# Transposes by age, five and six early blocks, and down's rows and residual tiles between units

## The chip, the core and the metric

The kernel runs on one core of a Trainium2 chip. The metric is the device time of one execution in microseconds (us). Before the change it is 2997.43 us, the median of three runs (2996.47 to 3000.92).

## What is computed

A diffusion trunk of two layers over 1024 latent tokens and, in the first layer only, 256 context tokens, model width 1024. Cut to what matters here:

```python
for l in range(2):
    p, qn, kn, vn, qg, kg, vg = project(x * (1 + s1) + sh1, w_in[l])
    mix = concat([pool(p), neighbourhood_attention(...), blocked_gqa(...)]) @ w_out[l]
    x = layer_norm(alpha * x + g1 * mix, ln1_g[l], ln1_b[l])
    ffn = conv_ffn(x * (1 + s2) + sh2, w_up[l], conv_w[l], conv_b[l], w_down[l])
    x = layer_norm(alpha * x + g2 * ffn, ln2_g[l], ln2_b[l])
    # layer 0: the same for the context stream xc

def conv_ffn(h, w_up, conv_w, conv_b, w_down):
    acc = conv3(h @ w_up) + conv_b          # along the tokens
    a, g = split(acc, 2)                    # 2816 columns each
    return (a * silu(g)) @ w_down
```

## The kernel before

All products are fp32 by three passes: each operand is split into a high and a low part (a cast on ScalarE, ACT, line L176 or L170, and a subtraction on VectorE, DVE, L177 or L172), and TensorE (PE) multiplies high by high, high by low and low by high. So each weight tile passes DMA, ACT and DVE before PE can use it. SyncE (SP) issues nearly all transfers in order; a transfer that waits for a tile holds those behind it. GpSimd (POOL) does some elementwise work.

A layer runs as: adaLN and in-projection, the three head groups, the out-projection with the first layer norm (class `OutProj`), `up` of the feed-forward part, `down` with the second layer norm. Layer 0 then runs the context stream's feed-forward part (`ffn`).

**Out-projection.** `OutProj.run` multiplies token tiles of 128 rows, 48 matmuls of 128x512 for each, into the PSUM tile `oacc` (L1072). PSUM holds four tiles of that size. The first tiles run k-major. `norm` of a tile multiplies by the gate into `s` (L1082, `SBUFS` buffers), sums with DVE (`ln_add`, L231), takes the variance on ACT and the power on POOL, applies it on ACT (L246), multiplies by the gain on POOL (L262), adds the offset on DVE (L263) to give `xm`, and stores `s` to DRAM (`XS`). Then PE transposes `xm` in eight matmuls of 128x128 into `tps` (L252), which takes one of the same four PSUM tiles. `follow` decides when the transposes stand in PE's order, and starts norms while fewer than `NXM` are not yet transposed.

**Early blocks.** `up` is a seven-product (Strassen-like) scheme, class `UpLat`. It needs sums of the transposed tiles named T1, T2 and T4, made from latent tiles 4 to 7 in `OutProj.sums`; they go to DRAM (`TX2`, `TX14`) and are loaded again in `enter`. Two of the products (24 of a block's 84 matmuls) need only the first four tiles. For `AHEAD` blocks they run ahead, as `early` (tile `oe`), while the last tiles are normed and transposed. `end` writes the order out by hand: "T" is a transpose, "E" an early block. Results of early blocks 2 and up go to DRAM (`UE`) and return before their block. The first product that needs a sum is `o<-T2`, which starts `up` proper.

**Down.** `DownLat.run` does seven products of 11 units; a unit loads a half tile of the hidden state (L1586) and one of the weights (L1592), splits both, and runs 12 matmuls. Between units it pops work from `self.later`. The residual tile is loaded (`s<-XS`, L1645 for tiles 0 to 3, L1655 for 4 to 7), multiplied by a row and added to another on DVE (`residual`, L1735, whose operations the trace gives to the helper's line L1329). The rows (`ln_g`, `ln_b`, `g`; in layer 1 also `l2g` and `l2b`) are loaded ahead of `run` (L224). A scheduler places instructions; what is not pinned may go earlier.

**Context feed-forward part.** `ffn` ends with `ln_add` and `modulate_T` for two tiles, then `tps`, then layer 1's projection.

Of the kernel before, what the change touches and what calls it, by code (L numbers as in the profile page):

```python
# [19 lines left out]
DEPTH = 2  # L20
# [13 lines left out]
NXM = (2, 3)  # L34
# [11 lines left out]
AHEAD = (4, 4)  # L46
# [30 lines left out]
YQ = 1  # L77
# [20 lines left out]
def trunk_kernel(ctx, tc, a, out):  # L98
# [51 lines left out]
    UE = {(l, f): dram.tile([P, 1024], F32, name=f"UE{l}{f}") for l in range(DEPTH) for f in range(2 * NP)}  # L150
    TX2 = dram.tile([4, P, 512], F32, name="TX2")
    TX14 = dram.tile([4, P, 1024], F32, name="TX14")
# [75 lines left out]
    def ln_add(s, o, pool, junk, apply=True):  # L228
# [6 lines left out]
        nc.vector.tensor_scalar(out=nm, in0=sm, scalar1=-1.0 / D, scalar2=None, op0=ALU.mult)  # L235
        sq = pool.tile([P, 1], F32, tag="lsq", name="lsq", bufs=LNB)
# [85 lines left out]
    def project_begin(l, wx1, ps, z, xt):  # L322
# [8 lines left out]
        for k in range(8):  # L331
            for i in range(len(accs)):
                accum_mm(xt, i, uA, 512, accs[i], k)
# [713 lines left out]
    class OutProj:  # L1047


        def __init__(self, l, units, op, ps):  # L1050
            self.l, self.units, self.op, self.ps = l, units, op, ps
            self.xs, self.stored, self.side = None, [], None
            self.rows = {}
            self.silu = False
            self.norms, self.late = [], []
# [21 lines left out]
        def norm(self, z, mx, t, acc, xin, x1_dst):  # L1077
# [6 lines left out]
            ln_add(s, xt, op, xt)  # L1084
            if SILU and not self.silu:
# [3 lines left out]
            sink = (lambda pt: self.sums(mx, t - 4, pt)) if z.lat and t >= 4 else None  # L1089
            self.late.append(  # L1090
                modulate_T(
                    s, G, B, op, "xm", NXM[self.l], self.ps, mx[0][:, t], mx[1][:, t], ident, False, mul=nc.gpsimd,
                    sink=sink,
                )
            )
            (nc.scalar if XQ else nc.sync).dma_start(out=x1_dst[t * P:(t + 1) * P, :], in_=s)

        def sums(self, mx, t, pt):
# [16 lines left out]
            else:  # L1115
                self.stored.append(t)
                nc.sync.dma_start(out=TX2[t], in_=r[:, hi])
                nc.sync.dma_start(out=TX14[t][:, lo], in_=q[:, lo])
            tt(nc.gpsimd, q[:, hi], q[:, hi], r[:, hi], ALU.subtract)
            nc.sync.dma_start(out=TX14[t][:, hi], in_=q[:, hi])  # L1120
# [8 lines left out]
        def run(self, z, tiles, mx, xin, x1_dst, kmajor=False, hold=False):  # L1129
# [5 lines left out]
            if kmajor:  # L1135
                for t in tiles:
                    acc(t)
                for k in range(7):
                    for t in tiles:
                        self.product(mx, accs[t], t, k)  # L1140
                    if self.side:
                        self.side()
            for t in tiles:
                if kmajor:
                    self.product(mx, accs[t], t, 7)
                else:
                    acc(t)
                    for k in range(8):
                        self.product(mx, accs[t], t, k)
                self.norms.append((z, mx, t, accs[t], xin, x1_dst))  # L1150
                if not kmajor and not (hold and t == tiles[-1]):
                    self.follow()
            if kmajor:
                while self.norms and len(self.late) < NXM[self.l]:
                    self.norm(*self.norms.pop(0))

        def end(self, cover, steps):

            while self.norms:
                self.norm(*self.norms.pop(0))  # L1160
            for x in steps:
                (self.late if x == "T" else cover).pop(0)()
# [43 lines left out]
    def ffn(l, z, mx, fp, ffp, ps, cols, g2, background, x1, lnrows, tail, ready, end=None, firstp=None):  # L1206
# [50 lines left out]
        def down(g, fs, F, last):  # L1257
            units = [wunit(a["wdown"][l, f], scale=g2) for f in fs[:3]]
            units += [wunit(a["wdown"][l, f], pool=fp, scale=g2, tags=("tmp", "tmp"), bufs=nb) for f in fs[3:]]
            for t in range(nt):  # L1260
# [24 lines left out]
                else:  # L1285
                    direct = end and t >= DIRECT
                    r = ln_add(s, o, fp, fp.tile([P, D], BF16, tag="junk", name="junk"), not direct)
                    tail(t, s, *(r or ()))
# [42 lines left out]
    class UpLat:  # L1331
# [36 lines left out]
        def enter(self, fu, xs, stored, background, t4=lambda fu: quarters(fu, ("T4",))[0]):  # L1368

            self.fu, self.xs, self.background = fu, xs, background  # L1370
            v = lambda x: x.rearrange("p (k j) -> p k j", k=4)

            def x(src):
                t = fu.tile([P, 1024], F32, tag="cv", name="xt", bufs=CVB)
                nc.sync.dma_start(out=t[:, :src.shape[1]], in_=src)
                return t
            xs.append(t4(fu))
            for t in stored:
                y = x(TX2[t])
                split(xs[1][0][:, t], xs[1][1][:, t], v(y[:, 0:512]))  # L1380
                y = x(TX14[t])
                split(xs[0][0][:, t], xs[0][1][:, t], v(y[:, 0:512]))
                split(xs[2][0][:, t], xs[2][1][:, t], v(y[:, 512:1024]))
            for t in range(4):
                if t not in stored:
                    y = x(TX14[t][:, 512:1024])
                    split(xs[2][0][:, t], xs[2][1][:, t], v(y[:, 0:512]))
# [6 lines left out]
        def weights(self, f, first=False):  # L1394
# [5 lines left out]
            elif b["early"] is None:  # L1400
                b["early"] = self.uf.tile([P, 1024], F32, tag="ue", name="ue", bufs=2)
                nc.sync.dma_start(out=b["early"], in_=UE[self.l, f])
                b["u1"] = b["early"][:, lo]
# [10 lines left out]
        def early(self, i):  # L1414
# [6 lines left out]
            u = self.uf.tile([P, 1024], F32, tag="ue", name="ue", bufs=2)  # L1421
            nc.scalar.copy(u[:, 0:512], o[:, 0:512])
            self.mm(o[:, 512:1024], a_, 512, "B21", True)
            tt(nc.vector, u[:, 512:1024], o[:, 512:1024], u[:, 0:512], ALU.add)
            self.blocks[f] = {"early": u, "u1": u[:, 0:512]}
# [758 lines left out]
```

## Time and profile before

| what | value |
|---|---|
| median of three runs | 2997.43 us |
| profiled execution, its own time | 2999.13 us |
| its span | 2997.4 us |
| mean granted clock of PE | 0.971 |
| PE, DVE, ACT, POOL busy | 93%, 76%, 50%, 33% |
| out-projection to `up`, layer 0 | 610 to 801 us |
| `down`, layer 0, start | about 1251 us |
| out-projection to `up`, layer 1 | 2188 to 2328 us |
| `down`, layer 1, start | about 2777 us |

The profile gives for each stretch the busy time of each engine, PE's granted clock (1.00 is 2.4 GHz, 0.50 would be 1.2 GHz all the time) and the DMA share. "Waits" lists for whom an engine was idle. A timeline row gives start, length, engine, line, operation and, in brackets, the idle time ahead and what ended it.

### The profile page before, as it was taken

To read this page: it belongs to the slowest core of one execution; us is meant where nothing else is said; L and a number is where in the kernel's file an instruction comes from. 1 tells how busy PE (TensorE), PEld (TensorE's weight loads), DVE (VectorE), ACT (ScalarE), POOL (GpSimd) and SP (SyncE) were. 2 spreads that over 40 slices of the span, in tenths; PEclk is the share of its full clock that TensorE was granted. 3 is DMA by queue.
4 is the path that set the end of the run, shared out by engine and by line. 5 is a ranking of instruction groups with operands and counts; after the bars stand their busy time and mean duration, and the time that the engine had idled before them with its cause. 6 is when DMAs were issued, how large, how long until landed. Compare 5 with 4: busy or idle time off the path is not lost.

```text
span 2997.4 us, 41914 instructions
## 1 busy us (share of the span) xinstructions
PE 2784.9 (93%) x14715; PEld 2359.7 (79%) x14715; DVE 2285.8 (76%) x3651; ACT 1492.3 (50%) x2328; POOL 991.3 (33%) x773
## 2 busy tenths in 40 slices
PE   8998889988799999899799799999998899999898
PEld 6798778977578887788788679888987688887676
DVE  4985789956688888756887765699957788887667
ACT  4222888824344444434655422598854444444343
POOL 0304354114345554200253440353133444553001
PEclk9999999998899999999899999999999999999999
DMA  7786662164554444865555588452134444445773
GB/s 275 249 269 192 184 169 85 43 219 154 190 168 155 154 152 158 292 211 185 181 177 183 186 269 289 142 171 83 58 121 137 161 158 158 157 159 179 264 222 129
DMA packets 271686, 531.08 MB, mean 177 GB/s; under 512 B 26778, under 2 KB 110834, under 8 KB 270708
## 3 DMA queue, kind: packets, MB, share of 16 engines
q1 hardware_dynamic: 270180, 524.11, 53.9%
q10 hardware_dynamic: 1296, 4.29, 0.4%
q8 instruction: 117, 1.92, 0.3%
q14 instruction: 93, 0.76, 0.1%
HBM read 394.16 MB, written 134.14 MB: 176 GB/s over the span
## 4 chain that ended last, share of the span: by engine, by line
PE 25%; DVE 15%; DMA 10%; issue 4%; ACT 4%; POOL 2%; SPq 1%; POOLq 0%; DVEq 0%; ACTq 0%
PE o L1363 7%; PE dy L1605 4%; PE dx L1605 3%; DVE wl L177 2%; PE pvs L848 2%; PE oacc L1072 2%; PE s L786 2%; DVE wl L172 2%; PE pt L803 1%; DVE s L1329 1%; DMA raw<-in_wup_dram 1%; DMA wm<-in_wmT_dram 1%; DMA VD<-stB 1%; DMA raw<-in_wdown_dram 1%; DVE w L1329 1%
## 5 line engine op out<-in xcount | busy, mean ns | idle before, releaser
L1329 POOL TENSOR_TENSOR cv<-cv 128x512 f32<-128x512 f32 (+1 forms) x110 | 251.5, 2286 | 262.5 <-DVE cv L1499 126.5
L1363 PE MATMUL o<-mxh,wh 128*128 128x512 f32 x640 | 253.5, 397 | 19.3 <-DVE cv L1499 12.7
L177 DVE TENSOR_TENSOR PT<-pt,PT 128x512 fp32r<-128x512 f32 (+2 forms) x396 | 247.8, 644 | 18.4 <-ACT PT L176 16.2
L1363 PE MATMUL o<-mxl,wh 128*128 128x512 f32 x640 | 252.6, 395 | 0.0
L1363 PE MATMUL o<-mxh,wl 128*128 128x512 f32 x640 | 251.6, 394 | 0.0
L786 PE MATMUL s<-K,q 128*128 128x256 f32 (+2 forms) x960 | 236.8, 359 | 14.6 <-DVE m L753 12.8
L176 ACT CAST wh<-raw 128x512 fp32r<-128x512 f32 (+1 forms) x132 | 119.0, 906 | 216.7 <-PE o L1363 141.1
L794 ACT ACTIVATE P<-P,m 128x1280 f32<-128x1280 f32 (+3 forms) x216 | 221.9, 1028 | 9.5 <-DVE m L753 8.0
L177 DVE TENSOR_TENSOR wl<-raw,wh 128x512 fp32r<-128x512 f32 (+1 forms) x132 | 162.8, 1239 | 75.7 <-ACT wh L176 75.1
L176 ACT CAST PT<-pt 128x512 fp32r<-128x512 f32 (+2 forms) x396 | 205.4, 558 | 26.0 <-PE pt L834 10.4
L848 PE MATMUL pvs<-PT,V 128*128 128x256 f32 (+1 forms) x1488 | 209.9, 289 | 5.0 <-DVE PT L177 2.0
L318 PE MATMUL pacc<-wh,mxh 128*128 128x512 f32 (+1 forms) x512 | 191.8, 375 | 15.5 <-DVE rt L284 7.2
L753 DVE CUSTOM_DVE_ANT_0 P<-s,zero,m 128x512 f32<-128x512 f32 (+1 forms) x288 | 189.0, 656 | 20.7 <-PE s L786 1.1
L172 DVE TENSOR_TENSOR wl<-raw,wh 128x1024 fp32r<-128x1024 f32 (+1 forms) x112 | 151.9, 1367 | 62.4 <-ACT wh L170 61.9
L848 PEld LDWEIGHTS pvs<-PT,V 128*128 128x128 f32 x1488 | 186.2, 191 | 12.2 <-ACT mixr L859 4.6
L320 PE MATMUL pacc<-wh,mxl 128*128 128x512 f32 (+1 forms) x512 | 187.5, 367 | 2.2 <-DVE mxl L177 2.2
L319 PE MATMUL pacc<-wl,mxh 128*128 128x512 f32 (+1 forms) x512 | 187.6, 366 | 0.0
L176 ACT CAST wh<-hw 128x1024 fp32r<-128x1024 f32 x98 | 102.7, 1053 | 160.8 <-PE dx L1605 37.5
L177 DVE TENSOR_TENSOR wl<-hw,wh 128x1024 fp32r<-128x1024 f32 x98 | 125.1, 1286 | 75.2 <-ACT wh L176 74.7
L170 ACT CAST wh<-raw 128x1024 fp32r<-128x1024 f32 (+1 forms) x118 | 119.1, 1018 | 93.4 <-POOL raw L168 23.6
L786 PEld LDWEIGHTS s<-K,q 128*128 128x128 f32 x960 | 140.8, 190 | 29.4 <-DVE m L753 23.1
L803 PE MATMUL pt<-ident,P 128*128 128x128 f32 x1032 | 160.1, 273 | 3.5 <-DVE PT L177 2.5
(355 smaller groups left out, 7849.1 us busy)
## 6 DMA issues: line engine op xcount, KB each, us to landing
raw<-in_wup_dram SPq DMA_DIRECT2D x140, 512.0 KB, 4.7
wm<-in_wmT_dram SPq DMA_DIRECT2D x96, 512.0 KB, 4.9
w<-in_wdown_dram SPq DMA_DIRECT2D x44, 512.0 KB, 3.7
hw<-in_wdown_dram SPq DMA_DIRECT2D x66, 256.0 KB, 3.7
q<-QN SPq DMA_DIRECT2D x96, 128.0 KB, 3.1
q<-QG SPq DMA_DIRECT2D x96, 128.0 KB, 2.7
TD0T<-w SPq DMA_DIRECT2D x44, 256.0 KB, 2.2
hw<-HD0S SPq DMA_DIRECT2D x44, 256.0 KB, 3.2
```

The lines of the kernel that those rows point to most:

```text
L172: (sub or nc.vector).tensor_tensor(out=lo[:, :n], in0=raw[:, :n], in1=h[:, :n], op=ALU.subtract)
L176: nc.scalar.copy(h, src)
L177: nc.vector.tensor_tensor(out=lo, in0=src, in1=h, op=ALU.subtract)
L318: nc.tensor.matmul(acc[:, :n], lhsT=xh[:, i, k, :], rhs=wh[:, o:o + n], start=(k == 0), stop=False)
L753: nc.vector.tensor_tensor_reduce(out=dst, in0=src, in1=bias, scale=-1.0, scalar=init, op0=ALU.add, op1=ALU.min, accum_out=m)
L786: nc.tensor.matmul(s[:, :n], lhsT=q[:, part, c0:c0 + P], rhs=K[:, k0:k0 + n], start=(part == 0), stop=(part == 1))
L794: nc.scalar.activation(out=self.P, in_=self.P, func=AF.Exp, bias=self.m, scale=-1.0, accum_out=self.rsum())
L803: nc.tensor.transpose(pt[:, b, :], self.P[:, p0 + b * P:p0 + (b + 1) * P], ident)
L848: nc.tensor.matmul(self.pv[:, c0:c0 + n], lhsT=V[:, vb, :], rhs=x[:, sl, c0:c0 + n], start=(self.c == 0), stop=(self.c == self.tot - 1),)
L1329: eng.tensor_tensor(out=out, in0=a_, in1=b_, op=op)
L1363: nc.tensor.matmul(o, lhsT=lhsT, rhs=rhs, start=fresh and k == 0 and i == 0, stop=k == 3 and i == 2, skip_group_check=not fresh,)
L1605: nc.tensor.matmul(o, lhsT=x[:, tc_], rhs=w[:, r], start=fresh and j == 0 and i == 0, stop=j == NP - 1 and i == 2, skip_group_check=not fresh,
```

## The change

- `OutProj`: `NXM` becomes 3 in both layers. `follow` is called in the middle and at the end of a tile and releases a transpose that is three steps old (`AGE`). The last latent tile and the context tiles take another route through the norm: the gain on DVE as soon as the mean is known, then one offset on DVE, instead of ACT, POOL and DVE in turn.
- `AHEAD` is (5, 6); all but one early block go through DRAM in halves of 512 columns, with `UEB` (3, 4) half buffers. The first half is stored from ACT's queue. "X" in `end` is `take`, which loads T1 and T2 while the early blocks run; `enter` loads T4 alone.
- `DownLat.run`: rows, then residual tiles 0 to 3, are loaded between units of product 1; tiles 4 to 7 in product 3; the residual operations run between units of products 2 and 4. Loads and operations are pinned in program order. Layer 1's `l2g` and `l2b` are asked for in the last norms, and the scheduler puts them into product 1.
- The context part's tail takes the gain and offset route. The stores of `YN` go from ACT's queue to SP's.
- The matmuls are the same in number.

```diff
-NXM = (2, 3)
+NXM = (3, 3)
-AHEAD = (4, 4)
+AHEAD = (5, 6)
+AGE = 3
+UEB = (3, 4)
-YQ = 1
+YQ = 0
...
+            if z.lat and t < 7:
+                ln_add(s, xt, op, xt)
+                f = modulate_T(s, G, B, op, "xm", NXM[self.l], self.ps, *dst, ident, False, mul=nc.gpsimd, sink=sink)
+            else:
+                xm = op.tile([P, D], F32, tag="xm", name="xm", bufs=NXM[self.l])
+                nm, rs = ln_add(s, xt, op, xt, False, lambda nm: gain(xm, s, nm, G))
+                offset(xm, xm, rs, B)
...
+                f = lambda: transpose_T(xm, self.ps, *dst, ident, False, sink)
+            self.late.append((self.step, f))
...
-        def follow(self, keep=1):
-            while len(self.late) > (keep if len(self.norms) < 2 else 0):
-                self.late.pop(0)()
+        def follow(self):
+
+            self.step += 1
+            if self.late and self.step - self.late[0][0] >= AGE:
+                self.late.pop(0)[1]()
             while self.norms and len(self.late) < NXM[self.l]:
                 self.norm(*self.norms.pop(0))
...
+        def take(self, proj, xs):
+
+            self.xs = proj.xs = xs
+            for t in proj.stored:
+                y = rawp.tile([P, 1024], F32, tag="raw", name="xt")
+                nc.sync.dma_start(out=y, in_=TX12[t])
+                for i in range(2):
+                    split(xs[i][0][:, t], xs[i][1][:, t], y[:, 512 * i:512 * i + 512].rearrange("p (k j) -> p k j", k=4))
...
-            return [lambda i=i: self.early(i) for i in [*range(2, n), 0, 1]]
+            return [lambda i=i: self.early(i) for i in [*range(1, n), 0]]
...
-                proj.end(up.cover(), "TETEETE")
+                proj.end(up.cover(), "ETEXTEEE")
...
-                proj.end(up.cover(), "ETEETE")
+                proj.end(up.cover(), "EXTEETEEE")
...
-                if j % 2 and self.later:
+                if (j % 2 or j and p in (1, 3)) and self.later:
                     self.later.pop(0)()
...
+            pin = tc.keep_in_program_order
+
+            def fetch(t):
+                return lambda: pin(nc.sync.dma_start(out=s[t], in_=x1[t * P:(t + 1) * P, :]))
             self.product(0, X, True, after=lambda t: nc.scalar.copy(u[t], X[t]))
-            self.later = [lambda t=t: residual(s[t]) for t in range(4)]
+            rows = {}
+            self.later = [
+                lambda: rows.update(ln=self.rows()), lambda: rows.update(g2=self.g2())
+            ] + [fetch(t) for t in range(4)]
...
+            self.later += [lambda t=t: residual(rows["ln"], s[t]) for t in range(4)]
             self.product(2, X, False, after=c11)
-            self.later = [lambda t=t: residual(s[t]) for t in range(4, 8)]
+            self.later += [fetch(t) for t in range(4, 8)]
...
+            self.later += [lambda t=t: residual(rows["ln"], s[t]) for t in range(4, 8)]
             self.product(4, X, True, after=c22)
```

PE's order where layer 0's out-projection transposes its first tiles. Before, the two transposes come after five tiles of `oacc`:

```order
2560 L1072 MATMUL oacc<-wh,mxh 128x512 x2
2561 L1072 MATMUL oacc<-wl,mxh 128x512 x2
2562 L1072 MATMUL oacc<-wh,mxl 128x512 x2
2563 L252 MATMUL tps<-ident,xm 128x128 x16
2564 L1072 MATMUL oacc<-wh,mxh 128x512 x2
2565 L1072 MATMUL oacc<-wl,mxh 128x512 x2
2566 L1072 MATMUL oacc<-wh,mxl 128x512 x2
```

These sixteen are the second pair of transposes, tiles 2 and 3, after six tiles. In the change the same place holds the first pair, tiles 0 and 1:

```order
2559 L1078 MATMUL oacc<-wh,mxh 128x512 x2
2560 L1078 MATMUL oacc<-wl,mxh 128x512 x2
2561 L1078 MATMUL oacc<-wh,mxl 128x512 x2
2562 L258 MATMUL tps<-ident,xm 128x128 x16
2563 L1078 MATMUL oacc<-wh,mxh 128x512 x2
2564 L1078 MATMUL oacc<-wl,mxh 128x512 x2
2565 L1078 MATMUL oacc<-wh,mxl 128x512 x2
```

So the first transposes stand one tile of 48 matmuls later.

SP's order at the start of layer 1's `down`, product 1 (`hw` are units' halves; `g`, `ln_g`, `ln_b`, `l2g`, `l2b` are rows). Before:

```order
1075 L1592 DMA hw<-TD1T_170 128x512
1076 L224 DMA g_26151<-rows1lat_17792 128x1024
1077 L224 DMA ln_g<-in_ln_g_dram 128x1024
1078 L224 DMA ln_b<-in_ln_b_dram 128x1024
1079 L224 DMA l2g<-in_ln_g_dram 128x1024
1080 L224 DMA l2b<-in_ln_b_dram 128x1024
1081 L1645 DMA s_26172<-XS_100 128x1024
1082 L1645 DMA s_26173<-XS_100 128x1024
1083 L1645 DMA s_26174<-XS_100 128x1024
1084 L1645 DMA s_26175<-XS_100 128x1024
1085 L1586 DMA hw<-HD1S_162 128x512
```

In the change:

```order
1101 L228 DMA ln_g<-in_ln_g_dram 128x1024
1102 L228 DMA ln_b<-in_ln_b_dram 128x1024
1103 L228 DMA g_26486<-rows1lat_17818 128x1024
1104 L1601 DMA hw<-HD1S_162 128x512
1105 L1607 DMA hw<-TD1T_170 128x512
1106 L1663 DMA s_26226<-XS_100 128x1024
1107 L228 DMA l2g<-in_ln_g_dram 128x1024
1108 L1601 DMA hw<-HD1S_162 128x512
1109 L1607 DMA hw<-TD1T_170 128x512
1110 L1663 DMA s_26227<-XS_100 128x1024
1111 L1601 DMA hw<-HD1S_162 128x512
1112 L1607 DMA hw<-TD1T_170 128x512
```

Nine transfers in a row became groups of one to three between units; the loads of tiles 4 to 7 left this stretch for product 3.

DVE's order at the same place (`mxl` and `wl` are low parts of units). Before:

```order
3295 L177 TENSOR_TENSOR wl<-hw,wh 128x1024 x3
3296 L1329 TENSOR_TENSOR s_26172<-s_26172,ln_g 128x1024
3297 L1329 TENSOR_TENSOR s_26172<-s_26172,ln_b 128x1024
3298 L1329 TENSOR_TENSOR s_26173<-s_26173,ln_g 128x1024
3299 L1329 TENSOR_TENSOR s_26174<-s_26174,ln_g 128x1024
3300 L1329 TENSOR_TENSOR s_26173<-s_26173,ln_b 128x1024
3301 L1329 TENSOR_TENSOR s_26175<-s_26175,ln_g 128x1024
3302 L1329 TENSOR_TENSOR s_26174<-s_26174,ln_b 128x1024
3303 L177 TENSOR_TENSOR mxl<-hw,mxh 128x1024
```

In the change:

```order
3311 L181 TENSOR_TENSOR wl<-hw,wh 128x1024 x3
3312 L181 TENSOR_TENSOR mxl<-hw,mxh 128x1024 x8
3313 L181 TENSOR_TENSOR wl<-hw,wh 128x1024 x2
3314 L1760 TENSOR_TENSOR s_26226<-s_26226,ln_g 128x1024
3315 L1343 TENSOR_TENSOR u_26218<-dy_26433,u_26218 128x512
3316 L181 TENSOR_TENSOR wl<-hw,wh 128x1024
3317 L1343 TENSOR_TENSOR u_26220<-dy_26434,u_26220 128x512
3318 L1760 TENSOR_TENSOR s_26226<-s_26226,ln_b 128x1024
3319 L181 TENSOR_TENSOR mxl<-hw,mxh 128x1024
```

Ten more splits stand ahead of the first residual operation, and splits stand between the residual operations.

## Rows read from the trace of the kernel before

**Rows 1.** The page's part 1, whole span (busy us, share, instructions).
```profile
PE 2784.9 (93%) x14715; PEld 2359.7 (79%) x14715; DVE 2285.8 (76%) x3651; ACT 1492.3 (50%) x2328; POOL 991.3 (33%) x773
```

**Rows 2.** Windows (busy us and count by engine, PEclk, DMA share, GB/s), three stretches of 20 us.
```profile
780.00:800.00 20.00, 6.71 (x14) 4.35 (x14) 12.25 (x14) 7.20 (x12) 6.42 (x4) 0.66 0.89 342
...
1280.00:1300.00 20.00, 20.00 (x90) 16.57 (x89) 11.43 (x12) 8.42 (x9) 0.00 (x0) 1.00 0.70 241
...
2320.00:2340.00 20.00, 13.72 (x49) 10.01 (x48) 15.55 (x20) 7.45 (x13) 6.44 (x4) 0.83 0.60 218
```

**Rows 3.** Waits of PE, 651 to 802 us (us in total, times, longest).
```profile
PE tps L252 <- DVE xm L263: 19.3, 5, 13.3
PE o L1363 <- ACT T2h L176: 8.8, 1, 8.8
PE oe L1363 <- ACT ue L1422: 5.5, 2, 4.7
PE tps L252 <- DVE lnm L235: 3.7, 1, 3.7
```

**Rows 4.** Timeline of PE and DVE, layer 0's out-projection.
```profile
678.53 1.94 PE L252 MATMUL tps<-ident,xm 128*128 128x128 f32 x8 [13.27 <-DVE xm L263]
...
680.00 1.22 DVE L1082 TENSOR_TENSOR s<-oacc,g 128x1024 f32<-128x1024 f32 x1 [1.61 <-DMA XS<-s]
```

**Rows 5.** Waits of PE, 801 to 860 us, and 2327 to 2420 us.
```profile
PE o L1363 <- ACT u L1443: 3.3, 1, 3.3
...
PE o L1363 <- ACT u L1443: 1.8, 1, 1.8
```

**Rows 6.** Waits of PE, 1244 to 1290 us.
```profile
PE dy L1605 <- ACT wh L176: 4.9, 1, 4.9
PE dy L1605 <- DVE wl L177: 4.0, 2, 2.6
```

**Rows 7.** Windows, start of `down`, layer 0.
```profile
1240.00:1260.00 20.00, 14.61 (x60) 10.92 (x58) 10.75 (x10) 8.72 (x12) 0.00 (x0) 0.94 1.02 366
1260.00:1280.00 20.00, 16.32 (x59) 12.91 (x60) 18.83 (x17) 5.26 (x5) 0.00 (x0) 0.81 0.69 223
```

**Rows 8.** Waits of PE, 1690 to 1705 us; ACT's and DVE's timeline there.
```profile
PE tps L252 <- DVE xm L263: 7.6, 1, 7.6
...
1693.25 2.37 ACT L246 ACTIVATE acc<-acc,lnb,lrs 128x1024 f32<-128x1024 f32 x2
...
1694.52 2.36 DVE L262 TENSOR_TENSOR xm<-acc,ln_g 128x1024 f32<-128x1024 f32 x2
```

**Rows 9.** Waits of PE, 2215 to 2330 us.
```profile
PE tps L252 <- DVE xm L263: 9.0, 3, 3.6
PE o L1363 <- ACT T2h L176: 6.0, 1, 6.0
PE oe L1363 <- ACT ue L1422: 2.1, 2, 1.4
```

**Rows 10.** Waits of PE, 2770 to 2870 us.
```profile
PE dy L1605 <- ACT mxh L176: 8.5, 1, 8.5
PE dy L1605 <- DVE mxl L177: 4.5, 2, 2.6
```

**Rows 11.** Windows, start of `down`, layer 1.
```profile
2780.00:2800.00 20.00, 10.25 (x42) 7.63 (x40) 11.09 (x10) 8.26 (x11) 0.00 (x0) 0.84 0.97 359
2800.00:2820.00 20.00, 16.73 (x59) 13.23 (x60) 17.74 (x16) 4.42 (x5) 0.00 (x0) 0.82 0.61 214
2820.00:2840.00 20.00, 20.00 (x90) 16.57 (x89) 13.23 (x13) 10.32 (x10) 0.00 (x0) 1.00 0.74 235
```

**Rows 12.** Timeline of SP and DVE, the same stretch.
```profile
2780.62 4.50 SPq L1645 DMA_DIRECT2D s<-XS  x4
...
2793.76 2.96 SPq L1655 DMA_DIRECT2D s<-XS  x4
...
2791.26 1.22 DVE L1329 TENSOR_TENSOR s<-s,ln_g 128x1024 f32<-128x1024 f32 x1 [8.33 <-DMA s<-XS]
```

More of the change, by code (lines that the diff above doesn't have):

```diff
@@ L225, in row_tile, with ln_add @@
         return t
-    def ln_add(s, o, pool, junk, apply=True):
+    def ln_add(s, o, pool, junk, apply=True, early=None):
         sm = pool.tile([P, 1], F32, tag="lsum", name="lsum", bufs=LNB)
@@ L1137, in run @@
                     acc(t)
-                for k in range(7):
+                for k in range(8):
                     for t in tiles:
@@ L1142, in run, with end @@
                         self.side()
+                self.norms += [(z, mx, t, accs[t], xin, x1_dst) for t in tiles]
+                self.follow()
+                return
             for t in tiles:
-                if kmajor:
-                    self.product(mx, accs[t], t, 7)
-                else:
[L1147 to L1162, printed above, removed]
+                acc(t)
+                for k in range(8):
+                    self.product(mx, accs[t], t, k)
+                    if k == 3:
+                        self.follow()
+                self.norms.append((z, mx, t, accs[t], xin, x1_dst))
+                self.follow()
+        def end(self, cover, steps):
+            assert not self.norms
+            for x in steps:
+                if x == "T":
+                    self.late.pop(0)[1]()
+                elif x == "X":
+                    self.take()
+                else:
+                    cover.pop(0)()
             assert not self.late and not cover
@@ L1285, in down @@
                 else:
-                    direct = end and t >= DIRECT
-                    r = ln_add(s, o, fp, fp.tile([P, D], BF16, tag="junk", name="junk"), not direct)
-                    tail(t, s, *(r or ()))
+                    tail(t, s, o)
         def residual(t):
@@ L1366, in mm, with enter @@
                     )
[L1368 to L1383, printed above, removed]
+        def take(self, proj, xs):
[3 more added lines that the diff above has]
+                nc.sync.dma_start(out=y, in_=TX12[t])
+                for i in range(2):
+                    split(xs[i][0][:, t], xs[i][1][:, t], y[:, 512 * i:512 * i + 512].rearrange("p (k j) -> p k j", k=4))
+        def enter(self, fu, t4, background):
+            self.fu, self.background = fu, background
+            self.xs.append(t4)
             for t in range(4):
-                if t not in stored:
-                    y = x(TX14[t][:, 512:1024])
-                    split(xs[2][0][:, t], xs[2][1][:, t], v(y[:, 0:512]))
+                y = fu.tile([P, 1024], F32, tag="cv", name="xt", bufs=CVB)
+                nc.sync.dma_start(out=y[:, 0:512], in_=TX4[t])
+                split(t4[0][:, t], t4[1][:, t], y[:, 0:512].rearrange("p (k j) -> p k j", k=4))
         def load(self, f, pool, tag, **kw):
@@ L1400, in weights @@
             elif b["early"] is None:
-                b["early"] = self.uf.tile([P, 1024], F32, tag="ue", name="ue", bufs=2)
-                nc.sync.dma_start(out=b["early"], in_=UE[self.l, f])
-                b["u1"] = b["early"][:, lo]
+                for i, n in enumerate(("u1", "early")):
+                    b[n] = self.half()
+                    nc.sync.dma_start(out=b[n], in_=UE[self.l, f][i])
             rg = self.load(NF + f, *((rawp, "raw") if first else (self.fu, "rg")), **({} if first else dict(bufs=2)))
@@ L1631, in product, with run @@
                 after(t)
-        def run(self, extra, tail, x1, residual, finish, late=None):
+        def run(self, extra, tail, x1, finish, late=None):
             self.extra, self.later = extra, []
-            fd, g2 = self.fd, self.g2
+            fd = self.fd
             lo, hi = slice(0, 512), slice(512, 1024)
@@ L1735, in residual @@
     def residual(rows, x):
-        tt(nc.vector, x, x, rows[0], ALU.mult)
-        tt(nc.vector, x, x, rows[1], ALU.add)
+        for r, op in zip(rows, (ALU.mult, ALU.add)):
+            tc.keep_in_program_order(nc.vector.tensor_tensor(out=x, in0=x, in1=r, op=op))
     att = []
@@ L1874, in trunk_kernel @@
                 proj.run(LAT, range(NKM[0], 8), *lat_args)
[L1875 removed]
+                proj.run(CTXS, range(2), mxc, xin(a["ctx"][0]), XSC)
                 wxs.close()
                 xss, xsp = right_pool("xs", 1)
[L1878 to L1879 removed]
+                proj.take = lambda: up.take(proj, quarters(xsp))
+                proj.end(up.cover(), "ETEXTEEE")
                 for i in range(2):
@@ L2063, in finish_o @@
             def finish_o(t, s, w):
+                if not last:
+                    last.extend(row_tile(fd, t_, a[nm][1]) for nm, t_ in (("ln2_g", "l2g"), ("ln2_b", "l2b")))
                 if t == LAT.nt - 1:
```

105 lines of the change are left out of this document (53 added, 52 removed).

## Prediction

> **What bounds the kernel.** I read the shares of the engines first, then the windows, then PE's waits in the stretches that the change touches, and last the timelines behind the longest of these waits. PE is busy 93% of the span [rows 1], so time is to be won only where PE waits, or where it runs at half clock behind a wait. The rate without waits is 90 matmuls of 128x512 in 20.00 us at clock 1.00, 0.222 us each [rows 2]; every cost in matmuls below goes by it. The losses lie in five places: the out-projection's end of each layer, the start of each `down`, and the context part's end.
>
> In layer 0's out-projection the longest wait is that of the first transposes for `xm`, 13.3 us [rows 3]; the timeline shows it as the 13.27 us ahead of 678.53 [rows 4]. Near its end PE waits 8.8 us for T2h, 5.5 for `ue` and 3.7 for a norm [rows 3], and from 780 to 800 us it issued 14 matmuls in 6.71 us of work at a mean clock of 0.66 [rows 2], part of the time at 1.2 GHz after having idled. Layer 1 has the same waits, smaller: 9.0, 6.0 and 2.1 us [rows 9].
>
> At the start of `down` two causes fall together. SP puts four residual tiles in a row ahead of a unit's halves and four more behind a few units [rows 12], so units come late; and DVE, in order, sits at the first residual operation for 8.33 us until its tile lands [rows 12], with splits queued behind it. PE waits 4.9 and 4.0 us in layer 0 [rows 6], 8.5 and 4.5 in layer 1 [rows 10].
>
> **The change, part by part.** The matmuls stay the same in number; what moves is what stands in PE's waits.
>
> *Layer 0, out-projection.* One more tile, 48 x 0.222 = 10.7 us, stands ahead of the first transposes. It can't all be won: with six tiles issued the first transposes need the PSUM tile that the third norm frees, and that norm read it from 680.00 to 681.22, after waiting for the store of `s` [rows 4]. So they start at about 681.3 in place of 678.5, and 10.7 - 2.8 = 8 us are won. Behind it, T1 and T2 are loaded and split while early blocks run, not after them, and a fifth block (24 x 0.222 = 5.3 us) stands there: I take the T2h wait, 8.8, as gone, and half of 5.5 + 3.7, that is 4.6. Of the 14 matmuls at low clock, 6.71 - 14 x 0.222 = 3.6 us were lost; half, 1.8, comes back. Against this stands a new round trip: SP now waits for the last tile's sums to be stored, loads them, and only then loads weights for the next early blocks. The trace doesn't show that wait. Its bounds are 0 and 8.8 us, the nearest row of a store, load and split that PE sat out [rows 3]; I take 4.4, since one or two blocks' matmuls lie between. Sum: 8 + 8.8 + 4.6 + 1.8 - 4.4 = 19 us (between 8, the first step alone, and 23).
>
> *Layer 1, out-projection.* Of the 9.0 us one wait of 3.6 for the last tile stays, 5.4 go; 6.0 and 2.1 go, since two more blocks (10.7 us) fill them [rows 9]. From 2320 to 2340 PE spent 13.72 us on 49 matmuls [rows 2], 2.8 more than at full rate; half comes back. Sum 5.4 + 8.1 + 1.4 = 15 us (between 5.4 and 17).
>
> *`up`'s first blocks.* A block whose early part is done leaves PE 60 matmuls, 13.3 us, in place of 84, while DVE, ACT and POOL still do its whole elementwise work. Now there are waits of 3.3 us in layer 0 and 1.8 in layer 1 [rows 5]. What an added such block costs, the trace doesn't show: between 0 and 3.3 us. I take 3 for layer 0's one, by its own row, and 2 each, 4, for layer 1's two, by theirs. The reloads of the halves count in a rival below.
>
> *Layer 0, `down`.* From 1240 to 1280 us PE issued 60 + 59 matmuls [rows 7] where 180 fit: 61 x 0.222 = 13.5 us lost at most. The change puts splits ahead of the residual operations and moves tiles 4 to 7 (4 x 0.52 = 2.1 MB) to product 3. The 40 us moved 20 x (366 + 223) = 11.8 MB [rows 7]; 9.7 MB stay, and at 366 GB/s they take 26.5 us, just what is left without the loss. So full recovery needs the best rate throughout, and I take two thirds, 9 us (between 4.0, the wait for DVE alone [rows 6], and 13.5).
>
> *Layer 1, `down`.* 42 + 59 matmuls in 40 us [rows 11] are 79 short, 17.5 us. Over 60 us the rows give 16.2 MB; without 2.1 MB, 14.1 in 42.5 us, 331 GB/s, under the 359 of the first window. More slack than in layer 0: three quarters, 13 us (between 4.5 [rows 10] and 17.5). In both layers the residual operations land in products 2 and 4, where POOL is idle and DVE, busy 13.23 of 20 us in a dense stretch [rows 11], takes eight operations of 1.22 us [rows 12] spread over some 22 us of matmuls.
>
> The Trainium skill, DMA: Bandwidth & Descriptors, section "Issuing engines are not separate DMA queues", says that all transfers run on the same 16 DMA engines and interleave, whichever engine issued them; by it an order of issue alone adds no bandwidth, only the 2.1 MB that leave the stretch count, and the time would be rival (a)'s, 2959. The trace agrees in the first window, whose DMA share is 1.02, and not in the second, 0.69 [rows 7], in which DVE was the busy one (18.83 of 20 us).
>
> *Context part's end.* The transposes wait 7.6 us for `xm`. Of the chain behind the variance, ACT's apply (2.37 for two, 1.2 for one) and DVE's gain (2.36 for two) leave [rows 8]: 1.2 + 2.4 = 3.6 at most, 3 taken (0 to 3.6). The stores of `YN` on SP and of half blocks on ACT cost nothing as long as SP is ahead; what they cost if it isn't belongs to the slower rival.
>
> **Sum.** -19 + 3 - 15 + 4 - 9 - 13 - 3 = -52 us. The profiled execution took 2999.13 us, so 2947.1; it lies 1.7 above the median of the runs, so **2945**.
>
> **Rivals.**
> (a) *Starved starts.* The start of `down` is bound by transfers: rows and tiles still move in product 1, and spreading them changes little. For it: the share of 1.02 and 366 GB/s. Against: the next windows, 0.61 to 0.69 [rows 7, 11]. Then only 4.0 and 4.5 us come back in place of 9 and 13: 2945 + 13.5 = 2959.
> (b) *Nothing is given back.* No new wait behind the last tile (4.4), no cost of the added blocks (7), both starts recovered in full (4.5 + 4.5): 2945 - 20 = 2925.
> (c) *Late sums.* `up` waits for the last tile's round trip wherever it stands, and the added blocks are bound by DVE. Then 8 and 5.4 us are won in the out-projections, 3.3 + 6.6 lost in the first blocks, 4.0 + 4.5 won in `down`, nothing at the context part: -12, so 2985.
> (d) *Slower: SP's queue is held at its head.* Four and five stored blocks return as 18 half tiles, through only three or four buffers, where four whole tiles returned before. A load whose buffer isn't free holds the weights behind it. If each holds PE as the longest wait for `ue` did, 4.7 us [rows 3], that is 85 us: 2945 + 85 = 3030. It decides from 52 / 18 = 2.9 us each. Against it: the loads stand several weight loads ahead of their use, and the waits of that kind cost 5.5 us in all.
> The Trainium skill, same page, section "Anatomy of one DMA — SWDGE (gpsimd) path", says that a semaphore wait is made by the issuing sequencer before dispatch, not by the DMA engines. That is the mechanism of (d); the rows show tiles issued in a row [rows 12] but no such stall of PE behind a reload.
>
> **How the numbers follow.** Forecast 0.55 (2932 to 2955), (a) 0.15, (b) 0.10, (c) 0.12, (d) 0.08. A measurement of this kernel tells about 0.2%, 6 us, from no change. Of (c), whose own spread reaches 2995, 0.04 counts as the same and 0.01 as slower. Faster 0.87, same 0.04, slower 0.09. The range goes from 2915, some 10 us past (b), to 2983, which takes in (a) and leaves out most of (c) and all of (d).
>
> **What would show it.** Right: the 13.3 us wait for `xm` down to about 5; `up` of layer 0 starting 19 us earlier; over 75 matmuls in each window at `down`'s start; no DVE idle on `s<-XS` over 2 us; 7 us more of waits in `up`'s first blocks. Wrong: fewer than 65 matmuls in these windows at a DMA share near 1 (a); an `o<-T2` wait of over 5 us (c); PE waiting for weights behind `ue` loads (d).

## The result, and the profile after

The changed kernel takes 2970.02 us in the median of three runs (2967.71 to 2974.76), before 2997.43. The ratio is 0.9898, with a 95% interval of 0.988 to 0.9917: 27 us faster, about half of the 52 that were forecast, and inside the stated range. The profiled execution is the median one; its span is 2968.2 us against 2997.4.

The first table says where the 29 us of span come from. Its marks are read off PE's timelines: the start of the first `oacc`, of the first product that needs T2, of the first `dx` and `dy` of a `down`, of the last of them, and of the first attention matmul. All times in us.

| stretch | before | after | difference | forecast |
|---|---|---|---|---|
| start to layer 0's out-projection | 610.6 | 608.3 | -2.3 | 0 |
| layer 0, out-projection to `down` | 598.7 | 590.8 | -8.0 | -19 + 3 |
| layer 0, `down`, from product 1 | 210.0 | 200.7 | -9.2 | -9 |
| context part and layer 1's projection | 463.9 | 468.1 | +4.2 | -3 |
| layer 1, out-projection to `down` | 551.7 | 549.8 | -2.0 | -15 + 4 |
| layer 1, `down`, from product 1 | 206.6 | 195.0 | -11.6 | -13 |

What is not listed (product 0 of `down`, attention) differs by 0.5 us or less. Stretches whose code is the same in several of the kernels below differ between their single profiles by 3 to 5 us (layer 0's out-projection to `down`: 590.8, 586.0, 586.4, 587.0), so a difference of that size in one profile says little. Each length here and below is that of one profile.

Both `down`s came about as forecast. The windows of the changed kernel, at the place of [rows 7] and [rows 11] (as far from the first `dy`, within 1 us):

```profile
1230.00:1250.00 20.00, 17.82 (x76) 13.73 (x75) 7.40 (x7) 10.14 (x12) 0.00 (x0) 1.00 0.93 336
1250.00:1270.00 20.00, 20.00 (x90) 16.55 (x89) 11.38 (x11) 8.42 (x8) 0.00 (x0) 1.00 0.79 259
2762.00:2782.00 20.00, 18.29 (x76) 13.76 (x76) 6.13 (x5) 9.66 (x12) 0.00 (x0) 1.00 0.99 370
2782.00:2802.00 20.00, 19.47 (x85) 15.59 (x84) 14.19 (x13) 9.73 (x10) 0.00 (x0) 1.00 0.74 237
```

76 and 90 matmuls stand where 60 and 59 stood, 76 and 85 where 42 and 59 stood, and the clock is 1.00. PE's waits there, 1234 to 1280 us and 2752 to 2850, the counterparts of [rows 6] and [rows 10]:

```profile
PE dy L1620 <- ACT wh L180: 1.5, 1, 1.5
PE dy L1620 <- DVE wl L181: 0.7, 1, 0.7
...
PE dy L1620 <- DVE mxl L181: 1.6, 3, 0.5
PE dy L1620 <- ACT mxh L180: 0.6, 1, 0.6
```

In place of 8.9 and 13.0 us, the two largest waits are 2.2 us together in each layer. SP now issues one tile between two units, where [rows 12] has four in a row:

```profile
2762.91 0.66 SPq L1663 DMA_DIRECT2D s<-XS  x1
...
2767.99 0.32 SPq L1663 DMA_DIRECT2D s<-XS  x1
```

The out-projections did not come as forecast. PE's waits from 651 to 800 us, the counterpart of [rows 3]:

```profile
PE oe L1377 <- ACT wh L180: 9.4, 1, 9.4
PE tps L258 <- DVE xm L269: 7.1, 3, 4.8
PE tps L258 <- DVE s L1088: 5.3, 2, 5.0
PE o L1377 <- ACT wh L180: 2.3, 1, 2.3
PE oe L1377 <- ACT ue L1432: 2.3, 1, 2.3
PE oacc L1078 <- DVE lnm L239: 1.5, 1, 1.5
PE o L1377 <- DVE wl L181: 0.9, 1, 0.9
```

The 13.3 us ahead of the first transposes became 5.0, and their releaser is now the norm whose `s<-oacc` frees a PSUM tile, as was worked out ahead. The T2h wait is gone. But an early block waits 9.4 us for its weights, and the seventh tile's transposes 4.8 us for `xm`. SP's timeline tells why the weights are late:

```profile
751.98 0.32 SPq L1387 DMA_DIRECT2D xt<-TX  x1
756.73 0.32 SPq L1129 DMA_DIRECT2D TX<-xq  x1
757.38 0.32 SPq L1439 DMA_DIRECT2D UE<-ue  x1
760.45 0.32 SPq L1130 DMA_DIRECT2D TX<-xr  x1
...
763.00 0.50 SPq L1387 DMA_DIRECT2D xt<-TX  x1
763.56 1.19 SPq L1401 DMA_DIRECT2D raw<-in_wup_dram  x2
```

The last tile's transposes ran at 739.42. SP then stands at the stores of its sums until VectorE has made them, 756.73 and 760.45, and the two weight loads behind them leave at 763.56. It is not the round trip that takes the time (from the store of `xr` to the load that needs it: 2.6 us) but the stores that wait at the queue's head. And VectorE is late with the sums since GpSimd's part of them, the first, had to wait for the one buffer `xq`, which the store of the tile before held:

```profile
752.61 2.41 POOL L1343 TENSOR_TENSOR xq<-mxh,mxl 128x1024 f32<-128x1024 f32 x1 [5.42 <-DMA TX<-xq]
```

That holds the first of the two sums. Ahead of the second, VectorE runs other operations for 3 us (756.68 to 759.75). A second `xq` in layer 0 was not tried.

At the context part's end the forecast's wait did shrink, and the next one grew. PE's waits, 1670 to 1705 us, beside [rows 8]:

```profile
PE pacc L324 <- DVE rt L290: 8.2, 1, 8.2
PE tps L258 <- DVE xm L1740: 4.8, 1, 4.8
```

The wait for `xm` fell from 7.6 to 4.8; behind it PE waits 8.2 us for `rt` (a tile of the projection's key norm), where the trace of before, in the same place, has:

```profile
PE pacc L318 <- DVE rt L284: 4.9, 1, 4.9
```

### The profile page after: what moved, and what is told of

Same layout as the page of the kernel before. It is cut to its first block, busy times and chain, and to the rows that moved or that the text cites. A ratio compares the mean times of both kernels' runs of the same rounds, so it can differ in the third digit from the quotient of the medians.

```text
span 2968.2 us, 41958 instructions
## 1 busy us (share of the span) xinstructions
PE 2781.8 (94%) x14715; PEld 2353.6 (79%) x14715; DVE 2295.3 (77%) x3656; ACT 1490.5 (50%) x2329; POOL 978.4 (33%) x769
## 5 line engine op out<-in xcount | busy, mean ns | idle before, releaser
L1377 PE MATMUL o<-mxh,wh 128*128 128x512 f32 x616 | 243.5, 396 | 10.4 <-DVE cv L1514 7.0
L1377 PE MATMUL o<-mxh,wl 128*128 128x512 f32 x616 | 241.8, 393 | 0.8 <-DVE wl L181 0.8
L1377 PE MATMUL o<-mxl,wh 128*128 128x512 f32 x616 | 242.5, 394 | 0.0
L800 ACT ACTIVATE P<-P,m 128x1280 f32<-128x1280 f32 (+3 forms) x216 | 221.8, 1027 | 10.1 <-DVE m L759 8.4
L324 PE MATMUL pacc<-wh,mxh 128*128 128x512 f32 (+1 forms) x512 | 191.4, 374 | 17.5 <-DVE rt L290 10.1
L854 PEld LDWEIGHTS pvs<-PT,V 128*128 128x128 f32 x1488 | 186.7, 191 | 12.3 <-ACT mixr L865 4.7
```

Of the source, the lines that this page charges most:

```text
L324: nc.tensor.matmul(acc[:, :n], lhsT=xh[:, i, k, :], rhs=wh[:, o:o + n], start=(k == 0), stop=False)
L800: nc.scalar.activation(out=self.P, in_=self.P, func=AF.Exp, bias=self.m, scale=-1.0, accum_out=self.rsum())
L854: nc.tensor.matmul(self.pv[:, c0:c0 + n], lhsT=V[:, vb, :], rhs=x[:, sl, c0:c0 + n], start=(self.c == 0), stop=(self.c == self.tot - 1),)
L1377: nc.tensor.matmul(o, lhsT=lhsT, rhs=rhs, start=fresh and k == 0 and i == 0, stop=k == 3 and i == 2, skip_group_check=not fresh,)
```

## Experiments

All change the changed kernel in one or two places. The times are medians; the ratio is to the kernel before, run beside them.

**1. Down as before.** The rows ahead of `run`, tiles 0 to 3 in product 0, their residual operations in product 1, the rest likewise, and no pins:

```diff
-            self.later = [
-                lambda: rows.update(ln=self.rows()), lambda: rows.update(g2=self.g2())
-            ] + [fetch(t) for t in range(4)]
+            self.later = [lambda t=t: residual(rows["ln"], s[t]) for t in range(4)]
```

> The changed kernel with down as it was before: rows and tiles loaded ahead and in a row, nothing pinned. If down's new order is what won its share (theory), layer 0's and layer 1's down take about 9 and 12 us longer again and the time is about 2991 us. If the starts were bound by transfers and the gain came from elsewhere (rival a), down keeps its new length within 3 us and the time stays near 2970.

2991.09 us, ratio 0.9979 (0.9969 to 0.9989). The two `down`s take 209.6 and 209.7 us again. In layer 0 the wait of before is back:

```profile
1238.55 1.23 DVE L1758 TENSOR_TENSOR s<-s,ln_g 128x1024 f32<-128x1024 f32 x1 [6.40 <-DMA s<-XS]
```

So `down`'s new form (order, places and pins together) carries 21 us of the 27, and rival (a), by which spreading the transfers changes little, is out.

**2. Down in its new place, not pinned.**

```diff
-                return lambda: pin(nc.sync.dma_start(out=s[t], in_=x1[t * P:(t + 1) * P, :]))
+                return lambda: nc.sync.dma_start(out=s[t], in_=x1[t * P:(t + 1) * P, :])
...
-            tc.keep_in_program_order(nc.vector.tensor_tensor(out=x, in0=x, in1=r, op=op))
+            nc.vector.tensor_tensor(out=x, in0=x, in1=r, op=op)
```

> The changed kernel with down's loads and residual operations where they now stand in the program, but not pinned: the scheduler then puts all sixteen residual operations of a layer close together again at product 1's start, and the loads of tiles 4 to 7 with those of 0 to 3. If the pins carry the gain, both downs lose most of the 9 and 12 us: 2985 to 2991. If loading the rows and tiles between units is enough, they lose under a third: 2970 to 2976.

2989.65 us, ratio 0.9976 (0.9963 to 0.9988): 211.5 and 209.9 us, nothing is left. No residual operation waits for its tile any more, but they stand close together again, and so do the loads of all eight tiles. In layer 0 PE waits for splits behind the residual operations (1225 to 1290 us), in a stretch in which VectorE is busy 18.93 of 20 us and the DMA share is 0.62:

```profile
PE dy L1620 <- DVE wl L181: 8.9, 2, 5.0
...
1247.00:1267.00 20.00, 14.78 (x46) 11.36 (x47) 18.93 (x18) 5.61 (x6) 0.00 (x0) 0.74 0.62 218
```

Without the pins nothing of the gain is left. In layer 0 VectorE's wait for a transfer is removed here and the time stays: the order on DVE is a cause of its own. The pins of the loads and those of the residual operations were not tried apart.

**3. Four early blocks in layer 1.** `AHEAD = (5, 4)`, with two "E" fewer.

> The changed kernel with four early blocks in layer 1 in place of six. Theory: up's first blocks there are held by work that an early block does not take away, so what two more blocks win ahead of up is given back in it; up of layer 1 then starts some 8 to 10 us later in its work but down of layer 1 starts within 3 us of the change: 2967 to 2973 us. The forecast's terms (a block fills 5.3 us of waits and costs 2): 5 to 8 us slower, 2975 to 2978.

2955.98 us, ratio 0.9862 (0.9842 to 0.9882). Neither theory: 14 us faster than the change in the medians. The two intervals just touch (0.9882 and 0.9880), but the slowest execution here, 2957.95 us, lies under the change's fastest, 2967.71. Layer 1's out-projection to `down` takes 536.7 us in place of 549.8. The matmuls of that stretch are the same; counting PE's idle time and the matmuls that start over 0.3 us behind the one ahead without idling, it is 19.7 us and 39 matmuls against 24.0 and 77.

**4. Four in both layers.** `AHEAD = (4, 4)`.

> The changed kernel with four early blocks in both layers. Theory: an early block wins 5.3 us ahead of up and pays it back in up's first blocks, where PE's part of a block falls from 84 to 60 matmuls while the elementwise chain keeps its length; so layer 0's fifth block is worth nothing either: down of layer 0 starts within 3 us of the change, the time is that of five and four, 2953 to 2959. The forecast's terms (5.3 won, 3 paid in layer 0): 2 to 3 us slower than five and four.

2951.26 us, ratio 0.9853 (0.9829 to 0.9877), clear of the change's interval. Layer 0's stretch takes 588.6 us, within the spread of the kernels with five (586 to 591): the fifth block is worth nothing that these runs can tell. Layer 1's takes 532.9.

**5. Three in layer 1.** `AHEAD = (5, 3)`.

> The changed kernel with three early blocks in layer 1. If each block beyond what the waits ahead of up can hold costs 6 us (two cost 13 to 14), and four are just what they hold, then three leave a wait of PE ahead of the first product that needs T2, 3 to 6 us, and win back some of it in up: 2955 to 2961, not better than four. If early blocks cost more than they win in any number, three are 4 to 7 us faster than four: 2949 to 2952.

2953.45 us, ratio 0.9859 (0.9835 to 0.9883). Between the two readings: layer 1's stretch takes 535.5 us, as with four.

**6. T1 and T2 loaded later.** The steps "ETETEXEE" and "EEXTETEEE".

> The changed kernel with the step that loads T1 and T2 again put one or two early blocks later (ETETEXEE, EEXTETEEE). Theory: in layer 0 the weights of the third early block are late by 9.4 us since SP holds them behind stores of the last tile's sums, which wait for VectorE; with the loads of sums behind those weights, the wait of PE for them falls under 4 us and the time by 4 to 8 us, 2962 to 2966. Rival: the chain of the last tile's sums itself is late, so the wait moves to the first product that needs T2 and the time stays within 3 us of 2970.

2963.81 us, ratio 0.9882 (0.9854 to 0.9909), which overlaps the change's. The wait for weights is gone as the theory has it, and the wait for buffers of half blocks, 2.3 us in the change, grew instead:

```profile
PE oe L1377 <- ACT ue L1432: 9.2, 3, 4.6
```

Unclear with five blocks; run 10 has the same with four.

**7. Side work in layer 1's projection pinned behind the key chunks.** GpSimd multiplies and adds to eight tiles from YN there (`side`), which the scheduler puts as early as it can. The key chunks are the loop over `chunk_A`, the projection's first.

```diff
-                nc.sync.dma_start(out=x, in_=YN[t * P:(t + 1) * P, :])
-                nc.gpsimd.tensor_tensor(out=x, in0=x, in1=prev[0], op=ALU.mult)
+                keep = tc.keep_in_program_order
+                keep(nc.sync.dma_start(out=x, in_=YN[t * P:(t + 1) * P, :]))
+                keep(nc.gpsimd.tensor_tensor(out=x, in0=x, in1=prev[0], op=ALU.mult))
```

> The changed kernel with the projection's side work in layer 1 (eight tiles loaded from YN, multiplied and added to on GpSimd) pinned to its place in program order, behind the key chunks. Theory: the 8.2 us wait for rt behind the context part's end comes from GpSimd's queue, whose small power operation stands behind six tile operations of 1.2 to 2.4 us, and takes back what the shorter norm chain won; pinned, the wait falls under 2 us and the time by 6 to 9 us, 2961 to 2964. Rival: the wait is for the rows' loads, then it stays and the time is unchanged; or the side work becomes late at the projection's end, then the time grows by up to 10 us.

2993.01 us, ratio 0.9986 (0.9974 to 0.9997). The 8.2 us for `rt` are gone, so it is the side work that held it. Through which queue is not shown. In the change GpSimd's small power operation, which `rt` needs, runs from 1699.67 to 1700.55, behind side operations of 2.4 us. But VectorE waits just before for a row, whose load SP issued at 1695.13 behind a store of the side work, and comes to `rt` at 1700.62 only:

```profile
1698.31 2.01 DVE L362 TENSOR_TENSOR Bk_norm<-cs,gn 128x256 f32<-128x256 f32 x2 [4.39 <-DMA gn<-in_k_norm_dram]
```

The run moves both, so the rival of the rows' loads is not out. The other rival came true, by more than its 10 us. From 1660 to 1900 us PE waits 15.2 us for weights and 13.5 for the split of `stC`:

```profile
PE pacc L324 <- ACT wh L174: 15.2, 2, 13.3
PE ktp L396 <- DVE stC L181: 13.5, 2, 7.6
```

The projection takes 269.4 us in place of 246.9.

**8. One side tile behind each key chunk.** The same pins, and `side(i)` called in the loop of the key chunks.

> The changed kernel with layer 1's side work in the projection pinned one tile behind each key chunk, in place of all of it at the start (the change) or all behind the key chunks (the run with the side work pinned later, whose rt wait fell to nothing but which lost over 20 us to late weights further on). Theory: GpSimd's queue holds rt; with one tile per chunk the 8.2 us wait falls under 3 and no new wait comes, so the projection is 5 to 8 us shorter than in the change: 2962 to 2965. Rival: any pinned side tile holds one of the three weight buffers at a bad time; then the projection is longer by over 5 us.

2958.51 us, ratio 0.9873 (0.9851 to 0.9895). The projection takes 242.0 us, 4.9 less than in the change; with the side work and the context tail as in the change it takes 245.4 to 248.1 in the other kernels. The intervals of the whole overlap. From 1660 to 1710 us what is left of the wait for `rt` is short:

```profile
PE tps L258 <- DVE xm L1740: 4.5, 1, 4.5
PE ktp L396 <- DVE stA L181: 1.9, 2, 1.4
PE ktp L396 <- DVE rt L290: 1.4, 1, 1.4
```

**9. The old context tail.** `ln_add` with its apply, then `modulate_T`.

> The changed kernel with the context part's last norm by the old route. The forecast gave the new route 3 us. Theory: it shortens the wait for xm by 2 to 3 us, but the wait for rt behind it is set by GpSimd's queue and grows by as much, so without it the transposes wait some 7.5 us again and rt some 5, and the time stays within 3 us of the change. If the forecast's term holds, it is 3 us slower.

2968.00 us, ratio 0.9904 (0.9884 to 0.9924). As the theory has it:

```profile
PE tps L258 <- DVE xm L269: 7.1, 1, 7.1
PE pacc L324 <- DVE rt L290: 5.8, 1, 5.8
```

12.9 us in sum, 13.0 in the change. The stretch from the end of layer 0's `down` to attention takes 468.4 us with the old tail and 468.1 with the new one.

**10. Both, and both with the later load.** Four blocks in both layers and one side tile behind each key chunk; then the same with "ETETEXE" in layer 0.

> The changed kernel with four early blocks in both layers and the side work one tile behind each key chunk. If what these two runs won adds up (four and four: some 19 us under the change in the median; the side work: 5 us in the projection itself), about 2946 us, between 2941 and 2950, faster than the change and than the kernel before. If the side work's run owed its time to another schedule of layer 1's up and not to the projection, it stays at 2950 to 2954.

> As the run with four and four and the side work in the key chunks, and in layer 0 T1 and T2 are loaded again one early block later (ETETEXE). If SP's held queue ahead of the early blocks' weights still costs 3 us or more with four blocks, 2 to 4 us under that run; if only buffers of half blocks take its place, within 2 us of it.

2954.16 us, ratio 0.9859 (0.9841 to 0.9878), and 2947.47 us, ratio 0.9847 (0.9826 to 0.9868). What runs 4 and 8 won did not add up: the projection keeps its gain (240.1 us), layer 1's stretch loses its own (542.2 and 539.6 us, against 532.9 in run 4). With the later load layer 0's stretch takes 580.1 us in place of 587.9. From 651 to 800 us:

```profile
PE tps L258 <- DVE xm L269: 6.7, 4, 3.2
PE oe L1377 <- ACT ue L1432: 5.1, 3, 3.3
...
PE o L1377 <- ACT wh L180: 4.2, 1, 4.2
```

The wait of an early block for weights, 10.1 us in the kernel without the later load, is gone; the waits for buffers grew from 2.1 to 5.1, those for the first full product's `wh` from 3.3 to 4.2. That is the theory of run 6. The last kernel is the fastest here, 50 us under the kernel before in the medians of its runs, and its interval ends below the change's; from run 4 it can't be told apart.

**11. YN stored by ACT.** `YQ = 1`.

> The changed kernel with the stores of YN issued by ACT, as before. The forecast put their move at nothing: the stretch from down's end in layer 0 to the projection (221 us in the change) then changes by under 2 us and the time stays within 4 us of 2970. If their stores hold SP ahead of the context part's weights, that stretch is 3 us shorter or more.

2961.78 us, ratio 0.9884 (0.9862 to 0.9905), which overlaps the change's; the profiled execution was the longest of its four, 2973.21. The stretch from `down`'s end to the projection takes 218.3 us in place of 221.2, but 217.3 to 220.6 in other kernels with the stores on SP. So the forecast's nothing stands within the spread, no better.

## Why the prediction was half right

**Right, in part by luck: the two starts of `down`.** 9 and 13 us were forecast; 9.2 and 11.6 came, and undoing them costs 21 (run 1). The mechanism holds: units and splits no longer queue behind tiles and residual operations. That the sizes fit so well is partly luck: "two thirds" and "three quarters" were choices, and the ten other kernels with this `down` take 202.4 to 204.4 us in layer 0 and 194.3 to 197.9 in layer 1, which is 5.6 to 7.6 and 8.7 to 12.3 won. The bytes argued the right way: at 0.93 and 0.99 the share of the transfers stays high in the first windows, and PE runs on. The Trainium skill (DMA: Bandwidth & Descriptors, "Issuing engines are not separate DMA queues") says that all transfers run on the same 16 DMA engines, whichever engine issued them; that share shows nothing against it. Rival (a), which the prediction worked out from it, gave the two starts 8.5 us, and 20.8 came. How much of that is the 2.1 MB that left the stretch and how much the order was not tried apart; in run 2's window above the order on VectorE is what holds PE. Run 2 adds what the working did not say: the new places win nothing unless they are pinned.

**Right in kind, wrong in size: layer 0's out-projection** (19 forecast, 3 given back). The first product that needs T2 comes 6.2 us sooner in the stretch, with 12 more matmuls (2.7 us) done: 8.9 of the 19. Behind it 1.0 is given back, not 3. The first step, 8 us, came: the wait fell by 13.3 - 5.0 = 8.3. The T2h wait went too, and of `ue` and the norm more than half. The step that failed is the new wait behind the last tile, put at 4.4 "since one or two blocks' matmuls lie between". It is 9.4. It was priced by the row of a round trip; what holds SP is not the round trip but the time until VectorE makes the sums, with the weights queued behind. Runs 6 and 10 remove it, at the price of waits for half buffers. Not in the sum at all are 2.3 and 0.9 us for the weights of the first full product. The waits for `xm` behind the first pair of transposes were left out too, 6.0 us before and 7.1 now. The change's 590.8 us is also the longest of the ten kernels with five blocks (585.6 to 590.8).

**Wrong: what added blocks win and cost in layer 1.** The step is "2 each, 4, for layer 1's two". Up to the first product that needs T2 the 15 us came nearly: that point comes 5.1 us sooner in the stretch, with 36 more matmuls (8.0 us) done, 13.1 in all. From there to `down` the change takes 415.5 us where the kernel before takes 412.3, with those 8.0 us of work already gone: 11 us given back, not 4.

The step ahead of it, by which "two more blocks (10.7 us) fill" the waits of 6.0 and 2.1, failed as well. With four blocks (run 3) that point comes 17.3 us sooner than in the kernel before, with 24 matmuls (5.3 us) fewer done: 12.0 in all. PE's waits in that part of run 3, 2172 to 2296 us, hold none for T2h:

```profile
PE oe L1377 <- ACT wh L180: 5.0, 1, 5.0
PE o L1377 <- ACT wh L180: 1.4, 1, 1.4
PE oe L1377 <- DVE wl L181: 1.0, 1, 1.0
PE o L1377 <- DVE T2l L181: 0.3, 1, 0.3
```

So the rest of the change wins nearly all of the 13 us, and the two blocks found little left to fill. Behind that point the change and run 3 take the same time, though the change has some 60 matmuls fewer to do there; its granted clock is lower (the change, then run 3):

```profile
2307.52:2722.97 415.45, 397.44 (x1682) 320.72 (x1680) 339.16 (x318) 179.33 (x211) 198.35 (x102) 0.97 0.48 161
...
2294.45:2709.08 414.63, 402.29 (x1741) 325.58 (x1741) 341.80 (x327) 183.29 (x217) 198.55 (x103) 1.00 0.49 165
```

PE's waits in the change's first blocks of `up`, 2307 to 2420 us, against the one of 1.8 us in [rows 5]:

```profile
PE o L1377 <- ACT wh L180: 3.9, 1, 3.9
PE o L1377 <- DVE cv L1514: 3.8, 2, 2.5
PE o L1377 <- ACT u L1458: 2.1, 1, 2.1
PE o L1377 <- DVE wl L181: 0.8, 1, 0.8
```

[rows 5] leaves out a second wait that the trace of before has in the same window:

```profile
PE o L1363 <- DVE cv L1499: 3.5, 1, 3.5
```

The price per block was taken from one wait of a kernel with four; it took the waits to grow by number and left out the half clock behind the longer ones. The longest is for late weights. SP's own waits, 2307 to 2420 us, say on what the weight loads wait:

```profile
SPq L1401 <- DVE wl L181: 34.4, 9, 7.5
...
SPq L1413 <- DMA ue<-UE: 2.2, 1, 2.2
```

The weight loads wait for the split that frees their buffer. The reloads of half blocks (L1413) wait 4.4 us in all, those of whole tiles in the kernel before 10.8 (2320 to 2420 us). That speaks against (d): SP was held, but little by those loads. That the weight loads' waits set the time is not shown: run 8 has 28.3 us of them with the same six blocks (2301 to 2415 us), and takes 406.2 us from there to `down`. Fewer blocks are better in runs 3, 4 and 5 (533 to 537 us).

What stays open: why layer 1's stretch takes 541.2 us with six blocks and pinned side work (run 8; its profile is the fastest of four executions), and 542.2 and 539.6 with four (run 10). The code there is that of the change and of run 4; only the schedule differs, and with it which of several waits of 1 to 5 us PE meets. By the traces, the change and runs 2, 7, 9 and 11 have one order of operations in this stretch, and take 549.1 to 550.5 us; run 1, also with six blocks, has a slightly different one and takes 549.4; runs 3 and 4 share another, both kernels of run 10 a third. Run 8's order of VectorE differs from the change's in a few operations only, from 20 us ahead of the first product that needs T2 to 4 us behind it. So six blocks cost 13 to 17 us against runs 3 and 4, and nothing against run 10; how much of that is the number of blocks and how much the order, and which instruction decides it, was not tried.

**Wrong: 3 us at the context part's end.** The step took the wait for `xm` as the last one. Run 9 shows the same sum of waits either way, since `rt` behind it is bound to the side work: a small power operation stands behind tile operations of 2.4 us in GpSimd's queue, and a row's load behind a store in SP's (run 7 removes the wait, run 8 most of it at no price in the projection). This was in the trace of before, 4.9 us one step further on.

By the first table the forecast's 52 us miss the span's 29 by 8 in layer 0's out-projection and `up`, 7 from the context part to attention (of which 4 lie within the spread of single profiles), 9 in layer 1's out-projection and `up` and 1 in its `down`; the 2 us that came ahead of the change's stretches go against these.

## What to carry to other kernels

A wait that is shortened is worth only what lies between it and the next wait on another queue; so before a chain is priced, follow its consumer one wait further. A store issued in order costs every load behind it the time until its data is made, which is not seen in any round trip. And work put ahead of a stage need not make the stage shorter, where the same chains run beside it (run 3 and the change: 415 us with some 60 matmuls' difference): price it by those chains, try fewer, and see whether the schedule changed as well.

## What the runs showed of the hardware

A VectorE operation on two SBUF tiles took 3.41 us just behind the start of a GpSimd operation; alone such an operation takes 1.22 [rows 12]. In the changed kernel's out-projection, DVE's and POOL's timelines:

```profile
707.68 3.41 DVE L269 TENSOR_TENSOR xm<-xm,B 128x1024 f32<-128x1024 f32 x1 [2.35 <-POOL xm L268]
```

```profile
707.61 2.40 POOL L268 TENSOR_TENSOR xm<-s,G 128x1024 f32<-128x1024 f32 x1
```

It begins 0.07 us behind GpSimd's operation, which ends at 710.01, and ends 1.1 us later, about as if it had started then. The Trainium skill, SBUF — State Buffer, says in section "Who interferes with whom" that a VectorE instruction with two SBUF inputs contends with a GpSimd one that reads SBUF, and in its summary for kernel authors that the second one to issue then waits until the first is done; these rows agree. The seventh tile's late `xm` ended with the same operation, 3.38 us long from 726.81, beside a GpSimd operation of 2.34 us from 726.77. The sum has no term for this.
